# Attention probabilities and merged rows split in SBUF and transposed by DMA, with new planner constants

## Chip, cores and metric

The kernel runs on one core of a Trainium2 chip. The metric is the device time of one execution in microseconds; lower is better. The time of the kernel before is the median of three runs, 1886.96 us (1886.47 to 1887.98).

## The reference

One step of a single-layer encoder over 1024 prompt frames and 32 sample frames of width 1024: a joint input projection, two parallel branches over 8 heads (differential attention and retention), their gated sum, an output projection, a SwiGLU block and a gated per-layer embedding.

```python
qa, ka, va, qr, kr, vr, g_ret, gate_a, gate_r = mix_inputs(x, w_in, ...)   # rmsnorm(x) @ w_in, split
s = jnp.einsum('bqhcd,bkhcd->bhcqk', q_blk, ka) * scale       # two softmax maps per head, c = 0, 1
p = jax.nn.softmax(jnp.where(mask, s, -jnp.inf), axis=-1)
a = p[:, :, 0] - lam * p[:, :, 1]
o = jnp.einsum('bhqk,bkhe->bqhe', a, va)                      # then rmsnorm over the head
...
mix = jax.nn.sigmoid(gate_a) * o_a + jax.nn.sigmoid(gate_r) * o_r
x = x + mix @ w_o
```

## The kernel before

**Arithmetic.** Matmuls keep about float32 accuracy with float16 operands: each operand is a pair, a high part (rounded to float16) and a low part (the rest), and one product takes three matmuls, high by high, high by low and low by high. Splitting a float32 tile into its pair takes two instructions: a scaled copy to float16 on ScalarE or VectorE, and a `scalar_tensor_tensor` on VectorE that multiplies and subtracts.

**Stages.** The first stage, 50 to about 1000 us of the trace, walks 8 heads of 9 units each (8 blocks of 128 prompt frames, and the sample as block 8): 72 units. For each unit `stream` projects two blocks of 512 columns (`project`, lines 748 to 750, 24 matmuls each), one for attention (`unit_a`, then `attend`) and, four units later (`LAG`), one for retention and gates (`unit_b`). The merged rows of a unit go to DRAM (`mix_d`) and come back as `mixs` for the output projection. Later stages (output projection, SwiGLU in 7 products, down projection, embedding gate) aren't touched.

**Attention of one unit** (`attend`). With NK keys (128 for block 0 up to 1024 for block 7; 544 for the sample) and `nb_` = 1 to 8 blocks of values (5 for the sample; 41 in a head): scores on PE into PSUM `sc` (889 to 892), row maximum (899, VectorE), two exponentials into the float32 tiles `pm[0]` and `pm[1]` of the pool `p`, which has 5 buffers (909, ScalarE), the two maps combined into `pm[0]` (923, VectorE). Then TensorE transposes each 128 x 128 block of `pm[0]` into PSUM (938), at most four to a bank; the bank is split into the high and low halves of `aT` (945 on ScalarE or 947 on VectorE, and 949); and the products with the values follow (957, 958, 961), three matmuls per block.

**End of a unit** (`unit_b`). The merged rows `mx` (1240) are transposed by TensorE (1245), split from PSUM into `mixT` (1250, 1252) and stored (1254).

**Transposing DMAs** already turn the queries and keys: the pair is made in SBUF as `qst`, and `nc.sync.dma_start_transpose` on SP's queue writes `q4` (1087, 128 rows x 256 columns, 64 KB) and `kT` (1088, 128 x 512, 128 KB).

**Order.** The instruction order on PE, DVE, ACT and POOL is fixed at build time by a planner, `Flow`: every piece of work is a generator that yields engine and assumed duration (`M` PE, `V` VectorE, `S` ScalarE, `G` GpSimd, `D` the DMA path), takes and returns buffers (`get`, `put`) and waits for events. `Flow` always issues the piece that could start first on its assumed clock. DMAs go to SP's single queue in the order in which the planner reaches them, and SP works through them strictly in order. For a transposing DMA the planner books `xbar(tiles)` on the DMA path and then `landed(tiles)` before the data may be used, a tile being 16 rows of 128 columns.

Of the kernel before, what the change touches and what calls it, by code (L numbers as in the profile page):

```python
# [21 lines left out]
P = 128  # L22
# [48 lines left out]
def M(us):  # L71
    return {"M": us}
# [6 lines left out]
def X(us):  # L79
    return {"D": us}  # L80


def xbar(tiles):

    return 0.5 + 0.027 * tiles


def landed(tiles):

    return ("delay", 2.0 + 0.03 * tiles)  # L90


def either(*ds):
    out = {}
    for d in ds:
        out.update(d)
    return out
# [100 lines left out]
def kernel(  # L198
# [26 lines left out]
    nc = tc.nc  # L225
# [30 lines left out]
    id32 = cst_sb[:, 0, :]  # L256
# [245 lines left out]
    with ExitStack() as pa:  # L502
# [18 lines left out]
        lsc = ca.tile([P, 1], F32, name="lsc")  # L521
# [5 lines left out]
        wk = pa.enter_context(DT(name="wk", bufs=2))  # L527
# [3 lines left out]
        ps_o = pa.enter_context(DT(name="ps_o", bufs=3, space=PSUM))  # L531
# [346 lines left out]
        def attend(key, i, R, q4, sblocks, masked, vblocks, NK, sc_ap, do_ap):  # L878
            pm, Z = [], sm(2, "Z", 6)
            nm = sm(2, "nm", 6)  # L880
            nb = sm(2, "nb", 6)
            for ms in ((0, 1),) if NK <= 512 else ((0,), (1,)):
# [3 lines left out]
                for m in ms:  # L886
                    for b0, n, kts in sblocks:
                        o = ps[0:R, 512 * ms.index(m) + b0:512 * ms.index(m) + b0 + n]
# [32 lines left out]
            p0, p1 = pm[0][0:R, 0:NK], pm[1][0:R, 0:NK]  # L921
            yield V(NK, 1.0, 0.06)
            nc.vector.scalar_tensor_tensor(out=p0, in0=p1, scalar=cz[0:R], in1=p0, op0=ALU.mult, op1=ALU.add)
            yield ("put", "p")
            yield V(1)
            dz = sm(1, "dz", 6)
            nc.vector.tensor_tensor(out=dz[0:R], in0=rz[0:R, 0:1], in1=do_ap[0:R], op=ALU.mult)
            nb_ = len(vblocks)
            yield ("get", "aT")
            aT = wk.tile([P, 2, 8, P], F16, tag="aT", name="aT")  # L930
            for j0 in range(0, nb_, 4):
                js = range(j0, min(j0 + 4, nb_))
                yield ("get", "o")
                yield M(0.107 * len(js))
                pt = ps_o.tile([P, 512], F32, tag="o", name="t").rearrange("p (b c) -> p b c", b=4)
                for j in js:
                    n = vblocks[j][0]
                    nc.tensor.transpose(out=pt[0:n, j - j0, 0:R], in_=pm[0][0:R, j * P:j * P + n], identity=id32[0:R, 0:R])  # L938
                if js[-1] == nb_ - 1:
                    yield ("put", "p")  # L940
                n, nj = vblocks[js[-1]][0], len(js)
                hi = aT[0:n, 0, j0:j0 + nj, 0:R]
                g = yield either(S(nj * R, 0.05), V(nj * R, 1.0, 0.06))
                if g == "S":
                    nc.scalar.activation(hi, pt[0:n, 0:nj, 0:R], AF.Copy, scale=lsc[0:n])
                else:
                    nc.vector.tensor_scalar(out=hi, in0=pt[0:n, 0:nj, 0:R], scalar1=lsc[0:n], scalar2=None, op0=ALU.mult)
                yield V(nj * R, 1.0, 0.06)
                nc.vector.scalar_tensor_tensor(out=aT[0:n, 1, j0:j0 + nj, 0:R], in0=pt[0:n, 0:nj, 0:R], scalar=lsc[0:n], in1=hi,
                                               op0=ALU.mult, op1=ALU.subtract)  # L950
                yield ("put", "o")
            yield ("get", "o")
            yield M(0.165 * nb_)
            po = ps_o.tile([P, 512], F32, tag="o", name="po")[0:R, 0:P]
# [70 lines left out]
        def unit_a(h, i, ps, dA, e):  # L1025
# [57 lines left out]
            yield ("get", "q4")  # L1083
            rows = st[0:R].rearrange("p g a c -> p (g a c)")
            q4 = wk.tile([P, 2, P], F16, tag="q4", name="q4")
            yield X(xbar(6 * RT // 16))
            nc.sync.dma_start_transpose(out=q4[:, :, 0:R], in_=rows[:, 0:256])
            nc.sync.dma_start_transpose(out=kT[:, :, t0:t0 + RT], in_=rows[0:RT, 256:768])
            yield landed(6 * RT // 16)
            yield ("put", "qst")  # L1090
            if i < NT - 1:

# [97 lines left out]
        def unit_b(h, i, ps, dB, e):  # L1190
# [47 lines left out]
            yield ("put", "th")  # L1238
            g = yield either(G(P), V(P))
            ENG[g].tensor_tensor(out=mx[0:R], in0=mx[0:R], in1=of[0:R], op=ALU.add)  # L1240
            yield ("delay", 0.4)
            yield ("get", "o")
            yield M(0.12)
            pt = ps_o.tile([P, 512], F32, tag="o", name="t")
            nc.tensor.transpose(out=pt[:, 0:P], in_=mx, identity=id32)
            pt = pt[:, 0:RT]
            yield ("get", "mix")
            yield S(P, 0.05)
            mt = hp.tile([P, 2, P], F16, tag="mixT", name="mixT", bufs=4)
            nc.scalar.activation(mt[:, 0, 0:RT], pt, AF.Copy, scale=smx)  # L1250
            yield V(P, 1.0, 0.06)
            nc.vector.scalar_tensor_tensor(out=mt[:, 1, 0:RT], in0=pt, scalar=smx, in1=mt[:, 0, 0:RT],
                                           op0=ALU.mult, op1=ALU.subtract)
            nc.sync.dma_start(out=mix_d[h, :, :, t0:t0 + RT], in_=mt[:, :, 0:RT])
            yield ("later", ("mix", 2.2))
            yield ("put", "o")
            yield ("put", "B")
            yield ("set", ("b", h, i))

# [118 lines left out]
        def stream():  # L1378
# [65 lines left out]
            for part in range(4):  # L1444
                flow.add(ple(part), 6)

        flow = Flow(dict(pj=3, sc=1, o=3, p=5, A=5, B=3, w=3, st=2, mix=4, z=3, kv=3, rot=2, sqz=2, qst=2, q4=2, aT=2, of=2,
                         ret=2, th=2, xc=3, su=1))
        flow.buffers["w"].pop()
        with tc.manual_schedule(engines={mybir.EngineType.PE, mybir.EngineType.DVE, mybir.EngineType.Activation,  # L1450
                                         mybir.EngineType.Pool}):
# [645 lines left out]
```

## Time and profile before

| | us |
|---|---|
| median of 3 runs | 1886.96 |
| profiled execution, its own time | 1889.55 |
| its span, first to last instruction | 1887.7 |
| PE busy | 1838.3 |
| DVE busy | 1487.0 |
| ACT busy | 1065.3 |
| POOL busy | 672.5 |

The profile lists for each group of instructions a line, an engine, the tile written and the tiles read, the count, the busy time and the mean length of one, and the idle time of the engine just before them. Consecutive matmuls overlap in their pipeline, so the mean length of one is longer than its share of PE's time; that share is read from the distance of two starts in the timeline. SP's own waits and issues stand in rows of SPq.

### The profile page before, as it was taken

The page shows a single profiled execution, that of the slowest core. Times are in us where ns is not written, and L with a number is a line of the kernel's source. Part 1 is how long each engine was busy: PE and PEld are TensorE (multiplying, and loading weights), DVE is VectorE, ACT ScalarE, POOL GpSimd, SP SyncE. Part 2 cuts the span into 40 slices and gives each one's busy share as a digit, 9 for nine tenths or more (in the row PEclk, how much of TensorE's full clock was granted, in tenths as well). Part 3 has the DMA queues.
Part 4 walks back from the last instruction along what each step waited for, and adds up shares of the span by engine and source line. Part 5 has one row for each costly group of instructions (what it writes and reads, how often), then busy time and mean ns, then how long its engine had stood idle before and what let it go on. Part 6 is the DMA issues. An engine that isn't in the chain of part 4 may idle for free.

```text
span 1887.7 us, 37668 instructions
## 1 busy us (share of the span) xinstructions
PE 1838.3 (97%) x13791; PEld 1196.6 (63%) x13791; DVE 1487.0 (79%) x3874; ACT 1065.3 (56%) x2776; POOL 672.5 (36%) x1137
## 2 busy tenths in 40 slices
PE   6999999999999999999999998999999999999999
PEld 3455555655655556555566686777777776666666
DVE  7888778778887888878887589999999986644364
ACT  7677667676676766767666345656555542201132
POOL 3555445454444454544441266323232300000010
PEclk9999999999999999999999999999999999999999
DMA  5333213123132231322218421222211116212031
GB/s 197 87 92 91 78 40 103 53 72 94 33 90 72 64 100 27 99 74 62 80 44 285 138 66 45 91 92 80 68 46 68 46 63 257 66 59 90 1 135 50
DMA packets 128780, 160.25 MB, mean 85 GB/s; under 512 B 82098, under 2 KB 108978, under 8 KB 120659
## 3 DMA queue, kind: packets, MB, share of 16 engines
q1 hardware_dynamic: 128594, 157.85, 26.6%
q8 instruction: 108, 1.77, 0.4%
q14 instruction: 78, 0.63, 0.1%
HBM read 113.09 MB, written 31.34 MB: 77 GB/s over the span
## 4 chain that ended last, share of the span: by engine, by line
PE 72%; DVE 14%; POOL 6%; ACT 4%; issue 3%; DMA 1%; SPq 0%; POOLq 0%; DVEq 0%; ACTq 0%
PE ps L488 9%; PE ps L489 9%; PE ps L490 9%; PE pj L748 7%; PE pj L750 7%; PE pj L749 7%; PE ps L1486 4%; PE ps L1484 4%; PE ps L1485 4%; PE t L938 1%; PE sc L889 1%; PE sc L892 1%; ACT p L909 1%; PE pj L759 1%; DVE w L1637 1%
## 5 line engine op out<-in xcount | busy, mean ns | idle before, releaser
L748 PE MATMUL pj<-w,xh 128*128 128x512 f16 x1024 | 389.1, 380 | 2.8 <-ACT w L479 2.8
L749 PE MATMUL pj<-w,xh 128*128 128x512 f16 x1024 | 389.0, 380 | 0.6 <-DVE w L481 0.6
L750 PE MATMUL pj<-w,xh 128*128 128x512 f16 x1024 | 388.9, 380 | 0.0
L489 PE MATMUL ps<-mixs,w 128*128 128x352 f16 (+1 forms) x960 | 262.1, 278 | 5.9 <-DVE mixs L1509 5.9
L488 PE MATMUL ps<-mixs,w 128*128 128x352 f16 (+1 forms) x960 | 262.1, 278 | 0.3 <-DVE o1c L244 0.3
L490 PE MATMUL ps<-mixs,w 128*128 128x352 f16 (+1 forms) x960 | 262.1, 278 | 0.0
L490 PEld LDWEIGHTS <-w 128*128 128x128 f16 x1736 | 170.7, 98 | 57.0 <-issue 6.0
L488 PEld LDWEIGHTS <-w 128*128 128x128 f16 x1736 | 171.0, 98 | 55.7 <-issue 4.9
L489 PEld LDWEIGHTS <-w 128*128 128x128 f16 x1736 | 170.7, 98 | 50.2 <-issue 1.2
L750 PEld LDWEIGHTS <-xh 128*128 128x128 f16 x1024 | 100.3, 98 | 122.5 <-issue 2.2
L1642 POOL TENSOR_TENSOR st<-st 128x512 f32<-128x512 f32 x66 | 88.9, 1347 | 244.4 <-DVE w L1637 165.7
L748 PEld LDWEIGHTS <-xh 128*128 128x128 f16 x1024 | 101.5, 99 | 79.2 <-issue 3.0
L749 PEld LDWEIGHTS <-xh 128*128 128x128 f16 x1024 | 100.2, 98 | 76.4 <-issue 3.7
L909 ACT ACTIVATE p<-sc,nb,scs 128x256 f32<-128x256 f32 (+7 forms) x128 | 106.0, 829 | 73.6 <-POOL nb L901 42.7
L488 PE MATMUL ps<-tT,w 128*128 128x352 f16 (+1 forms) x528 | 143.5, 276 | 0.0
L489 PE MATMUL ps<-tT,w 128*128 128x352 f16 (+1 forms) x528 | 143.4, 276 | 0.0
L490 PE MATMUL ps<-tT,w 128*128 128x352 f16 (+1 forms) x528 | 143.4, 276 | 0.0
L1637 DVE SCALAR_TENSOR_TENSOR w<-st,gus,w 128x512 f16<-128x512 f32 x132 | 138.2, 1047 | 0.1
L899 DVE TENSOR_REDUCE nm<-sc 128x1 f32<-128x640 f32 (+6 forms) x112 | 102.8, 918 | 15.5 <-PE sc L892 14.4
L1486 PE MATMUL ps<-a,w 128*128 128x352 f16 x312 | 97.5, 313 | 0.5 <-DVE w L1728 0.5
L1484 PE MATMUL ps<-a,w 128*128 128x352 f16 x312 | 97.5, 313 | 0.0
L1485 PE MATMUL ps<-a,w 128*128 128x352 f16 x312 | 97.5, 313 | 0.0
(427 smaller groups left out, 4741.7 us busy)
## 6 DMA issues: line engine op xcount, KB each, us to landing
st<-in_win_dram SPq DMA_DIRECT2D x30, 1024.0 KB, 5.0
st<-in_wgu_dram SPq DMA_DIRECT2D x22, 1024.0 KB, 4.9
st<-in_wdn_dram SPq DMA_DIRECT2D x16, 704.0 KB, 4.9
out_dram<-kv SPq DMA_DIRECT2D x64, 128.0 KB, 1.7
a_d<-a SPq DMA_DIRECT2D x9, 528.0 KB, 2.6
b<-a_d SPq DMA_DIRECT2D x9, 528.0 KB, 7.7
mixs<-mix_d SPq DMA_DIRECT2D x8, 528.0 KB, 7.1
pw_d<-pws SPq DMA_DIRECT2D x12, 352.0 KB, 5.1
```

The costliest lines, as they stand in the source:

```text
L488: nc.tensor.matmul(out=ps, lhsT=wh, rhs=ah, start=first, stop=False)
L489: nc.tensor.matmul(out=ps, lhsT=wh, rhs=al, start=False, stop=False)
L490: nc.tensor.matmul(out=ps, lhsT=wl, rhs=ah, start=False, stop=last)
L748: nc.tensor.matmul(out=ps, lhsT=xhi, rhs=w[:, k, 0], start=(k == 0), stop=False)
L749: nc.tensor.matmul(out=ps, lhsT=xhi, rhs=w[:, k, 1], start=False, stop=False)
L750: nc.tensor.matmul(out=ps, lhsT=xh[:, k, 1, t0:t0 + P], rhs=w[:, k, 0], start=False, stop=(k == KD - 1))
L899: nc.vector.tensor_reduce(out=nm[0:R, mc], in_=pv, axis=AX.X, op=ALU.max, negate=True)
L909: nc.scalar.activation(pt[0:R, 0:NK], ps[0:R, p0:p0 + NK], AF.Exp, bias=nb[0:R, m:m + 1], scale=sc_ap[0:R], accum_out=Z[0:R, m:m + 1])
L1484: nc.tensor.matmul(out=ps, lhsT=wt[:, 0, j], rhs=a[:, 0, cs], start=(first and j == js[0]), stop=False)
L1485: nc.tensor.matmul(out=ps, lhsT=wt[:, 1, j], rhs=a[:, 0, cs], start=False, stop=False)
L1486: nc.tensor.matmul(out=ps, lhsT=wt[:, 2, j], rhs=a[:, 1, cs], start=False, stop=(last and j == js[-1]))
L1637: nc.vector.scalar_tensor_tensor(out=w[:, i, 1], in0=src, scalar=s, in1=w[:, i, 0], op0=ALU.mult, op1=ALU.subtract)
```

## The change

In `attend`, the combined map in `pm[0]` is split in SBUF: the float16 halves go side by side into the memory of `pm[1]`, which is free once the maps are combined, and one transposing DMA turns all blocks, high and low, into `aT`. The 328 PE transposes of a run (41 for each of 8 heads) go, and 72 DMAs of 2 x `nb_` blocks come. `pm[1]` now returns to the pool only when the DMA has landed, `pm[0]` when the low half is written. In `unit_b` the merged rows are split into a new tile `ms` (2 buffers) and turned by a DMA of 64 KB; the 72 PE transposes go, and the store to `mix_d` waits for that DMA. The fixed delay of 0.4 ahead of the old transpose goes. The planner's `xbar` and `landed` get other numbers, for the query and key DMAs too, which are now booked as two pieces.

```diff
 def xbar(tiles):
-    return 0.5 + 0.027 * tiles
+    return 1.15 + 0.006 * tiles
 def landed(tiles):
-    return ("delay", 2.0 + 0.03 * tiles)
+    return ("delay", 1.3 + 0.02 * tiles)
@@ attend
+            NB = nb_ * P
+            pf = pm[1].bitcast(F16)
+            hi, lo, src = pf[0:R, 0:NB], pf[0:R, NB:2 * NB], pm[0][0:R, 0:NB]
+            g = yield either(S(NB, 0.05), V(NB, 1.0, 0.06))
+            if g == "S":
+                nc.scalar.activation(hi, src, AF.Copy, scale=lsc[0:R])
+            else:
+                nc.vector.tensor_scalar(out=hi, in0=src, scalar1=lsc[0:R], scalar2=None, op0=ALU.mult)
+            yield V(NB, 1.0, 0.06)
+            nc.vector.scalar_tensor_tensor(out=lo, in0=src, scalar=lsc[0:R], in1=hi, op0=ALU.mult, op1=ALU.subtract)
+            yield ("put", "p")
             yield ("get", "aT")
-            for j0 in range(0, nb_, 4):
-                yield M(0.107 * len(js))
-                for j in js:
-                    nc.tensor.transpose(out=pt[0:n, j - j0, 0:R], in_=pm[0][0:R, j * P:j * P + n], identity=id32[0:R, 0:R])
...
-                nc.vector.scalar_tensor_tensor(out=aT[0:n, 1, j0:j0 + nj, 0:R], in0=pt[0:n, 0:nj, 0:R], scalar=lsc[0:n], in1=hi,
+            yield X(xbar(2 * nb_ * R // 16))
+            nc.sync.dma_start_transpose(out=aT.rearrange("p a j c -> p (a j) c")[:, :, 0:R], in_=pf[0:R, 0:2 * NB])
+            yield landed(2 * nb_ * R // 16)
+            yield ("put", "p")
@@ unit_a
-            yield X(xbar(6 * RT // 16))
+            yield X(xbar(2 * R // 16))
             nc.sync.dma_start_transpose(out=q4[:, :, 0:R], in_=rows[:, 0:256])
+            yield X(xbar(4 * RT // 16))
             nc.sync.dma_start_transpose(out=kT[:, :, t0:t0 + RT], in_=rows[0:RT, 256:768])
-            yield landed(6 * RT // 16)
+            yield landed(4 * RT // 16)
@@ unit_b
-            yield ("delay", 0.4)
-            yield M(0.12)
-            nc.tensor.transpose(out=pt[:, 0:P], in_=mx, identity=id32)
+            nc.scalar.activation(ms[:, 0], mx, AF.Copy, scale=smx)
+            nc.vector.scalar_tensor_tensor(out=ms[:, 1], in0=mx, scalar=smx, in1=ms[:, 0], op0=ALU.mult, op1=ALU.subtract)
+            yield X(xbar(2 * RT // 16))
+            nc.sync.dma_start_transpose(out=mt[:, :, 0:RT], in_=ms[0:RT].rearrange("p a c -> p (a c)"))
+            yield landed(2 * RT // 16)
+            yield X(0.05)
             nc.sync.dma_start(out=mix_d[h, :, :, t0:t0 + RT], in_=mt[:, :, 0:RT])
```

Since the planner sets the order anew, rows move on every engine. Three places show it. First SP's queue in the third head, where blocks 5 and 6 are under way; of before (weight load, store of keys and values, the two DMAs of queries and keys, two stores of merged rows):

```order
L421 DMA st<-in_win_dram 128x2048
L1063 DMA out_dram<-kv 128x256
L1087 DMA_TRANSPOSE q_5354<-qst 128x2x128
L1088 DMA_TRANSPOSE kT<-qst 128x4x128
L1254 DMA mix_d<-mixT 256x1x128 x2
```

And of the changed kernel at that place (L942 turns the probabilities, with 2 x `nb_` as the middle size, L1244 the merged rows, L1248 stores them, L1056 stores keys and values):

```order
L942 DMA_TRANSPOSE aT<-p 128x10x128
L942 DMA_TRANSPOSE aT<-p 128x12x128
L1056 DMA out_dram<-kv 128x256
L1244 DMA_TRANSPOSE mixT<-ms 128x2x128
L1080 DMA_TRANSPOSE q_5464<-qst 128x2x128
L1082 DMA_TRANSPOSE kT<-qst 128x4x128
L1248 DMA mix_d<-mixT 256x1x128
L942 DMA_TRANSPOSE aT<-p 128x14x128
```

The queue holds two DMAs more for each unit, and the probabilities of one unit now stand behind stores and turns of other units. Over the whole program the store of merged rows stands directly behind its own transposing DMA in 28 of 72 units.

Second PE in the sixth head, around the products of block 0; of before:

```order
L750 MATMUL pj<-w,xh 128x512
L314 LDWEIGHTS cst_sb
L314 MATMUL mt<-wamh,cst_sb 128x1
L957 LDWEIGHTS aT
L957 MATMUL po<-vh,aT 128x128
L958 LDWEIGHTS aT
L958 MATMUL po<-vh,aT 128x128
L961 LDWEIGHTS aT
L961 MATMUL po<-vh,aT 128x128
L1245 MATMUL t<-cst_sb,mx 128x128
```

And of the changed kernel there (L950, L951 and L954 are the products):

```order
L750 MATMUL pj<-w,xh 128x512
L950 LDWEIGHTS aT
L950 MATMUL po<-vh,aT 128x128
L951 LDWEIGHTS aT
L951 MATMUL po<-vh,aT 128x128
L954 LDWEIGHTS aT
L954 MATMUL po<-vh,aT 128x128
L759 LDWEIGHTS w
```

The products are the same; no transpose stands among them any more, neither of merged rows (L1245) nor of probabilities.

Third DVE in the fifth head, block 2, from the combination of the maps to the low half; of before:

```order
L923 SCALAR_TENSOR_TENSOR p<-p,cz 128x384
L1169 TENSOR_TENSOR inn<-pr,cst_sb 128x128
L927 TENSOR_TENSOR dz<-rz,dop 128x1
L947 TENSOR_SCALAR aT<-t,lsc 128x384
L1181 TENSOR_TENSOR S_134<-s_136,pr 64x128
L949 SCALAR_TENSOR_TENSOR aT<-t,lsc,aT 128x384
```

And of the changed kernel:

```order
L923 SCALAR_TENSOR_TENSOR p<-p,cz 128x384
L1177 TENSOR_SCALAR S_134<-S_134 64x128
L926 TENSOR_TENSOR dz<-rz,dop 128x1
L1046 TENSOR_REDUCE qss<-sqz 128x4
L935 TENSOR_SCALAR p<-p,lsc 128x384
L1009 SCALAR_TENSOR_TENSOR vh<-pj,vh 128x128
L937 SCALAR_TENSOR_TENSOR p<-p,lsc 128x384
```

The split now reads and writes SBUF (`p`) where it read PSUM (`t`), and it comes in one piece of all columns: 72 low halves (L937) in place of 112, and 30 of the high halves on DVE (L935) with 42 on ACT.

More of the change, by code (lines that the diff above doesn't have):

```diff
@@ L923, in attend @@
             nc.vector.scalar_tensor_tensor(out=p0, in0=p1, scalar=cz[0:R], in1=p0, op0=ALU.mult, op1=ALU.add)
-            yield ("put", "p")
             yield V(1)
@@ L928, in attend @@
             nb_ = len(vblocks)
-            yield ("get", "aT")
-            aT = wk.tile([P, 2, 8, P], F16, tag="aT", name="aT")
-            for j0 in range(0, nb_, 4):
-                js = range(j0, min(j0 + 4, nb_))
-                yield ("get", "o")
-                yield M(0.107 * len(js))
-                pt = ps_o.tile([P, 512], F32, tag="o", name="t").rearrange("p (b c) -> p b c", b=4)
-                for j in js:
[L937 to L951, printed above, removed]
@@ L952, in attend @@
+            yield ("put", "p")
+            yield ("get", "aT")
+            aT = wk.tile([P, 2 * 8 * P], F16, tag="aT", name="aT")[:, 0:2 * NB].rearrange("p (a j c) -> p a j c", a=2, c=P)
+            yield X(xbar(2 * nb_ * R // 16))
+            nc.sync.dma_start_transpose(out=aT.rearrange("p a j c -> p (a j) c")[:, :, 0:R], in_=pf[0:R, 0:2 * NB])
+            yield landed(2 * nb_ * R // 16)
+            yield ("put", "p")
             yield ("get", "o")
@@ L1240, in unit_b @@
             ENG[g].tensor_tensor(out=mx[0:R], in0=mx[0:R], in1=of[0:R], op=ALU.add)
-            yield ("delay", 0.4)
-            yield ("get", "o")
-            yield M(0.12)
-            pt = ps_o.tile([P, 512], F32, tag="o", name="t")
-            nc.tensor.transpose(out=pt[:, 0:P], in_=mx, identity=id32)
-            pt = pt[:, 0:RT]
+            yield ("get", "ms")
+            yield S(P, 0.05)
+            ms = wk.tile([P, 2, P], F16, tag="ms", name="ms")
+            nc.scalar.activation(ms[:, 0], mx, AF.Copy, scale=smx)
+            yield V(P, 1.0, 0.06)
+            nc.vector.scalar_tensor_tensor(out=ms[:, 1], in0=mx, scalar=smx, in1=ms[:, 0], op0=ALU.mult, op1=ALU.subtract)
             yield ("get", "mix")
-            yield S(P, 0.05)
             mt = hp.tile([P, 2, P], F16, tag="mixT", name="mixT", bufs=4)
[L1250 to L1253, printed above, removed]
+            yield X(xbar(2 * RT // 16))
+            nc.sync.dma_start_transpose(out=mt[:, :, 0:RT], in_=ms[0:RT].rearrange("p a c -> p (a c)"))
+            yield landed(2 * RT // 16)
+            yield ("put", "ms")
+            yield X(0.05)
             nc.sync.dma_start(out=mix_d[h, :, :, t0:t0 + RT], in_=mt[:, :, 0:RT])
             yield ("later", ("mix", 2.2))
-            yield ("put", "o")
             yield ("put", "B")
@@ L1447 @@
         flow = Flow(dict(pj=3, sc=1, o=3, p=5, A=5, B=3, w=3, st=2, mix=4, z=3, kv=3, rot=2, sqz=2, qst=2, q4=2, aT=2, of=2,
-                         ret=2, th=2, xc=3, su=1))
+                         ret=2, th=2, xc=3, su=1, ms=2))
         flow.buffers["w"].pop()
```

## Prediction

> **What bounds the kernel now.** I read the page's busy shares and its 40 slices first, then a table by stretches of the first stage, then the groups of instructions.
>
> ```profile
> PE 1838.3 (97%) x13791; PEld 1196.6 (63%) x13791; DVE 1487.0 (79%) x3874; ACT 1065.3 (56%) x2776; POOL 672.5 (36%) x1137
> PE   6999999999999999999999998999999999999999
> 770.00:890.00 120.00, 118.62 (x850) 69.93 (x849) 98.76 (x300) 82.76 (x247) 55.68 (x117) 1.00 0.26 72
> 50.00:998.00 948.00, 932.73 (x6626) 547.51 (x6625) 778.97 (x2351) 655.76 (x1947) 454.05 (x927) 1.00 0.26 72
> ```
>
> The columns of the last two rows are the stretch, then PE, PEld, DVE, ACT and POOL busy, granted clock, DMA share and GB/s. In the stage that the change touches PE is busy 118.62 of 120 us at full clock, DVE 98.76, ACT 82.76, and the DMA engines a quarter. PE's order is fixed, so an instruction that goes from PE gives back its share of PE's time, as long as nothing else arrives later than PE then comes to it.
>
> **What goes from PE.** Start-to-start distances, since matmuls overlap:
>
> ```profile
> L938 PE MATMUL t<-cst_sb,p 128*128 128x128 f32 x328 | 54.4, 274 | 1.4 <-DVE p L923 1.1 <-DVE aT L949 0.2
> L1245 PE MATMUL t<-cst_sb,mx 128*128 128x128 f32 x72 | 20.5, 284 | 4.8 <-POOL mx L1240 2.7 <-DVE mx L1240 1.8
> 985.06 0.60 PE L938 MATMUL t<-cst_sb,p 128*128 128x128 f32 x4
> 985.49 0.38 PE L889 MATMUL sc<-kcs,q 128*128 128x512 f16 x1
> 644.71 0.28 PE L1245 MATMUL t<-cst_sb,mx 128*128 128x128 f32 x1
> 644.83 0.38 PE L748 MATMUL pj<-w,xh 128*128 128x512 f16 x1
> ```
>
> Four transposes take 985.49 - 985.06 = 0.43 us, 0.108 each; one of merged rows takes 0.12. So 328 x 0.108 + 72 x 0.12 = 35.4 + 8.6 = **44.0 us** of PE time go, and with them the listed idle time ahead of them, 1.4 + 4.8 = 6.2 us, which may come back at the next waiting instruction.
>
> **What DVE and ACT get.** The low half of the probabilities stays one DVE instruction per element, from SBUF in place of PSUM:
>
> ```profile
> L949 DVE SCALAR_TENSOR_TENSOR aT<-t,lsc,aT 128x512 f16<-128x512 f32 x54 | 40.0, 743 | 2.5 <-ACT aT L945 2.3
> L923 DVE SCALAR_TENSOR_TENSOR p<-p,cz 128x512 f32<-128x512 f32 x8 | 6.0, 750 | 0.2
> L923 DVE SCALAR_TENSOR_TENSOR p<-p,cz 128x1024 f32<-128x1024 f32 x8 | 10.3, 1284 | 0.2
> L909 ACT ACTIVATE p<-sc,nb,scs 128x1024 f32<-128x1024 f32 x16 | 19.2, 1201 | 4.4 <-POOL nb L901 4.4
> ```
>
> The form from SBUF costs the same at 512 columns (750 against 743 ns), and one of 1024 (1284) replaces two of 512 (1486), so DVE loses a little work, and with 30 instead of 54 high halves on it a little more. At 98.76 of 120 it has room for a head that is 5.5 us shorter (44.0 / 8). The merged rows keep their two instructions. I book nothing for DVE and ACT; PE hides both, and if it did not, DVE at 98.76 would only bind a stretch cut from 120 us to under 99.
>
> **What SP and the DMA engines get.** The kernel already has two transposing DMAs per unit, which give issue and landing:
>
> ```profile
> L1087 SPq DMA_TRANSPOSE q<-qst x72: 1167/1195/2177, 43.1 to 978.0; - x72
> L1088 SPq DMA_TRANSPOSE kT<-qst x72: 1170/1216/2066, 44.5 to 979.3; - x72
> q<-qst SPq DMA_TRANSPOSE x72, 2.3
> kT<-qst SPq DMA_TRANSPOSE x72, 2.4
> 645.95 1.21 SPq L1088 DMA_TRANSPOSE kT<-qst  x1
> 647.00:647.50 0.50, 0.50 (x4) 0.28 (x2) 0.48 (x2) 0.50 (x2) 0.00 (x0) 1.00 0.61 127
> 647.50:648.00 0.50, 0.50 (x6) 0.47 (x6) 0.35 (x1) 0.50 (x2) 0.00 (x0) 1.00 1.58 125
> ```
>
> SP is held 1.2 us by either, 64 or 128 KB, and they land 2.3 and 2.4 us after the issue began. A merged-row DMA is the size of `q`: 1.2 held, 2.3 to land. One of the probabilities has 64 KB per block of values, so 64 to 512 KB. No row shows 512 KB, so its landing is bounded: by the step from `q` to `kT` (0.1 us for 64 KB) it is 2.3 + 7 x 0.1 = 3.0 us; by the two stretches, in which the 128 KB of `kT` took about 1.0 us from about 1.05 us after its issue, it is 1.05 + 4 x 1.0 + 0.3 = 5.4 us. I take 3.9, nearer the landings measured whole. Load on the DMA engines: (0.61 + 1.58) x 0.5 = 1.1 us of all 16 for 128 KB; 41 x 64 KB + 9 x 64 KB = 3.2 MB per head make 27 us, some 24% of a head, on top of 0.26. Not a bound.
>
> The Trainium skill, "Advanced Engine Details and Errata", section X-Bar Transpose (TRN2), expects 350-400 GB/s; an estimate from it is 1.4 us of transfer for 512 KB, which would put the landing near the lower bound, where the stretches above show 127 GB/s over half a microsecond; the lower landing would raise the forecast's chance and leave its sum.
>
> **Does PE reach the products before the data?** The new chain from the last score to the products of block 7 (1024 keys), out of the rows above and these:
>
> ```profile
> L899 DVE TENSOR_REDUCE nm<-sc 128x1 f32<-128x1024 f32 x16 | 19.5, 1219 | 1.6 <-PE sc L892 1.5
> L909 ACT ACTIVATION_READ_ACCUMULATOR p<-sc,nb,scs 128x1 f32 x128 | 25.0, 195 | 0.0
> L919 DVE SCALAR_TENSOR_TENSOR cz<-rz,nlam,Z 128x1 f32<-128x1 f32 x71 | 18.6, 261 | 1.2
> L916 DVE RECIPROCAL rz<-Z 128x2 f32<-128x2 f32 x71 | 11.5, 162 | 29.1 <-ACT p L909 28.3
> L901 DVE TENSOR_SCALAR nb<-nm,scs 128x1 f32<-128x1 f32 x20 | 4.1, 206 | 0.2
> L899 DVE TENSOR_REDUCE nm<-sc 128x2 f32<-128x256 f32 x8 | 3.4, 422 | 1.9 <-PE sc L892 1.2 <-PE mt L314 0.6
> L909 ACT ACTIVATE p<-sc,nb,scs 128x128 f32<-128x128 f32 x16 | 7.3, 456 | 11.9 <-DVE nb L901 8.8 <-POOL nb L901 2.3 <-DVE B1p L248 0.8
> L923 DVE SCALAR_TENSOR_TENSOR p<-p,cz 128x128 f32<-128x128 f32 x8 | 2.9, 361 | 0.2
> 645.48 0.38 PE L748 MATMUL pj<-w,xh 128*128 128x512 f16 x1
> ```
>
> Maximum 1.22, bias 0.21, exponential 1.20 + 0.20, reciprocal and factor 0.42, combination 1.28, high half 1.20 (as an exponential of that width), low half 1.28, landing 3.9: 10.9 us, 10.0 to 12.4 by the bounds. Counting PE's rows between that unit's last score and first product in the new order, each at its start-to-start distance (0.217 for a projection, (645.48 - 644.83) / 3, and 0.108 for a float32 transpose), PE has 15.0 us of work there (median of heads 2 to 8, the least 11.2), against 12.0 before. For block 0 (64 KB) the same chain with the short forms (0.42 maximum, exponentials of 0.46 + 0.20 twice, 0.36 for each later step) makes about 6 us, and PE has 9.0 (8.0 at least) against 5.5 before. So the order leaves 3 to 4 us for queueing, where block 0 of before, with a chain of 3.7, had 1.8. And these were PE's waits in the stage at products and scores with that:
>
> ```profile
> PE sc L889 <- ACT p L909: 1.9, 2, 1.5
> PE po L957 <- DVE aT L947: 0.9, 1, 0.9
> PE po L957 <- DVE aT L949: 0.4, 1, 0.4
> ```
>
> In all 72 units the scores never waited on a landing. What the new wait at the products costs in all isn't shown: it is nothing if SP keeps the planner's order, and 72 times the mean overshoot if not. I take 0.1 us a unit, **7 us**, since the few waits above total 3.2 us and SP is now in the path. What stands behind a waiting product in PE's queue is the next projection, so an overshoot is lost in full.
>
> **The end of the stage.** The last merged rows now go through a DMA of 2.3 us in place of a transpose of 0.3 before the store and the reload. Before, the output projection began behind a weight load, not behind them:
>
> ```profile
> 1021.54 0.32 SPq L1376 DMA_DIRECT2D mixs<-mix_d x1
> 1025.96 0.69 DVE L440 TENSOR_REDUCE wam<-st 128x2 f32<-128x512 f32 x1 [3.49 <-DMA st<-in_wo_dram]
> 1030.89 0.47 PE L488 MATMUL ps<-mixs,w 128*128 128x352 f16 x1 [0.26 <-DVE o1c L244]
> ```
>
> I book 2 us; if all is hidden, 0. The table of issue and landing times for `q` and `kT` is part of the same order and costs nothing by itself.
>
> **Sum.** The profiled execution took 1889.55 us (span 1887.7), 2.6 above the median 1886.96. -44.0 - 6.2 + 7 + 2 = -41 us: 1848 beside the profile's time, **1846** beside the median.
>
> **Rivals.**
> 1. *Large turns are dear.* If SP's hold grows with size as bytes do, 512 KB hold SP 4 x 1.2 = 4.8 us and land no sooner than 6; the chain of block 7 becomes 7.0 + 6 = 13 of PE's 15.0, the queue has 2 us a unit more, and a mean overshoot that I put at 0.4 us in 72 units takes 29 us in place of the 7: 1846 + 22 = 1868. For it: no row shows a turn over 128 KB. Against: doubling the size cost 21 ns.
> 2. *SP's order turns on the change.* SP works in order, and behind a late item everything is late:
>
> ```profile
> SPq L1063 <- POOL kv L1062: 282.0, 59, 8.5
> SPq L1087 <- DVE qst L1077: 51.0, 39, 3.5
> ```
>
> The store of keys and values held SP 59 times, 282.0 / 59 = 4.8 us each; before, only work that came later anyway stood behind it. Now turned probabilities do, and a store of merged rows that waits 2.3 - 1.2 = 1.1 us for its own turn. A product caught behind both is 5.9 us late, less the 3 to 4 us of room: 2.4 us. If two units in three are caught, 48 x 2.4 = 115 us of stall stand against 48 us: 1886.96 - 50 + 2 + 115, about 1954; if half of that, 1896. It decides from a mean overshoot of 0.67 us a unit (48 / 72). For it: the numbers of the row. Against: in 39 units SP stood waiting for the queries themselves, so it kept up with the planner's order.
>
> The Trainium skill, "VectorE: DVE Perf Modes", Rules for kernel authors, speaks against the change: for a 128 x 128 transpose it names TensorE if PSUM will do, the crossbar otherwise. By that rule the longer path would show as waits, and the time would be rival 2's; the trace has 0.108 us of a busy PE against 2.3 us of a queue that scores have never waited for.
> 3. *The change doesn't do what it says*, because PE isn't the bound: then the stage stays 948 us long and the time within 0.2%. 118.62 of 120 us speaks against it.
>
> **How the numbers follow.** Forecast 1846 (1836 to 1857): 0.58; rival 1 (1857 to 1883): 0.20; rival 3 (same): 0.05; rival 2 (slower): 0.17. The low end is -50 with no new wait at all. With the high end at 1884, 0.22 lies above and some 0.01 below, so I reach a little into rival 3 and the mild half of rival 2: 1834 to 1892. Faster by over 0.2% (about what a measurement of this kernel can tell from no change) 0.78, within 0.05, slower 0.17.
>
> **What would show it.** Right: PE busy in the first stage again at 98 to 99% of a stage near 905 us; no transposes of probabilities in the list; waits of PE at the products (L950) under 10 us in all; probabilities landing 2.3 to 4 us after issue, SP held about 1.2 to 1.4 by each. Rival 1: SP held several microseconds by the large ones. Rival 2: waits at L950 of 50 us or more, and SP rows in which L942 stands behind L1056 or L1248. The forecast is wrong if PE's idle time in the stage exceeds some 20 us.

## The result, and the profile after

| | median, us | runs | ratio to before, 95% interval |
|---|---|---|---|
| before | 1886.47 | 1883.87 to 1887.98 (5) | |
| changed | 1896.78 | 1893.62 to 1899.95 (5) | 1.0058 (1.0042 to 1.0074) |

The changed kernel is 0.6% slower; the forecast was 2.2% faster. Its profiled execution took 1898.33 us with a span of 1896.5. First the busy time of each engine, its share of the span and its instructions, of the changed kernel:

```profile
PE 1808.5 (95%) x13391; PEld 1152.9 (61%) x13391; DVE 1474.4 (78%) x3784; ACT 1063.3 (56%) x2762; POOL 715.1 (38%) x1161
```

PE is 29.8 us less busy than in before (1838.3), and yet the span is 8.8 us longer: PE has got idle time. Where, the table by stretches tells. Its columns are the stretch, PE, PEld, DVE, ACT and POOL busy, granted clock, DMA share, GB/s. Before:

```profile
50.00:950.00 900.00, 884.77 (x6252) 517.11 (x6251) 739.09 (x2241) 625.30 (x1859) 436.25 (x886) 1.00 0.26 73
950.00:1050.00 100.00, 97.08 (x743) 63.33 (x742) 72.54 (x210) 58.41 (x159) 23.05 (x54) 0.97 0.55 185
```

Changed:

```profile
50.00:950.00 900.00, 851.73 (x5862) 474.58 (x5860) 722.70 (x2141) 621.80 (x1842) 473.79 (x906) 0.99 0.42 99
950.00:1050.00 100.00, 90.63 (x676) 55.73 (x674) 72.89 (x214) 58.56 (x161) 29.18 (x58) 0.95 0.63 185
```

Up to 950 us PE stands idle 900 - 851.73 = 48.3 us against 15.2, and at the end of the stage 9.4 against 2.9: 39.5 us of new idle time against 44.0 us of work removed. The clock is lower too. The prediction's own sign of being wrong, more than some 20 us of idle time in the stage, is there. The output projection, whose first matmul started at 1030.89 in before, starts here:

```profile
1038.95 0.47 PE L488 MATMUL ps<-mixs,w 128*128 128x352 f16 x1 [0.25 <-DVE o1c L244]
```

8.1 us later; what follows takes as long as before within 1 us, so the loss lies ahead of that row. Of PE's waits in the changed kernel (time in all, times, longest) the first row is the largest, and the second is the one that matters later:

```profile
PE po L950 <- DMA aT<-p: 23.9, 16, 4.5
...
PE sc L889 <- DMA kT<-qst: 3.1, 3, 1.3
```

How the DMAs of the probabilities issued (SP's hold in ns: least, median, most) and landed, from the view of that line:

```profile
L942 SPq DMA_TRANSPOSE aT<-p x72: 1175/1350/2691, 63.3 to 997.1; - x72
DMA to landing us min/median/max: 2.3/3.7/7.7
```

Sixteen products waited, 23.9 us in all. The longest of these waits, from the timeline of the changed kernel:

```profile
661.03 1.21 SPq L1080 DMA_TRANSPOSE q<-qst  x1
661.59 0.48 DVE L937 SCALAR_TENSOR_TENSOR p<-p,lsc 128x256 f16<-128x256 f32 x1
662.34 2.02 SPq L1082 DMA_TRANSPOSE kT<-qst  x1
664.45 0.54 SPq L421 DMA_DIRECT2D st<-in_win_dram  x1
665.08 1.20 SPq L942 DMA_TRANSPOSE aT<-p  x1
670.41 0.29 PE L950 MATMUL po<-vh,aT 128*128 128x128 f16 x1 [4.52 <-DMA aT<-p]
```

The low half was ready at 661.59 + 0.48 = 662.07. SP first turned keys (2.02 us) and issued a weight load of 1 MB, came to the probabilities 3.0 us late, and these took 5.3 us to land behind the load. Two causes offer themselves at once, a landing that is late behind a load and SP's order. They work together: of the sixteen turns that were waited for, SP came to thirteen more than 1 us after the low half was ready, and seven, with 14.9 of the 23.9 us, had a weight load issued less than 4 us ahead of them. The experiments try them one by one.

### The profile page after: what moved, and what is told of

It reads as the page before. It is cut to its first block, busy times and chain, and to the rows that moved or that the text cites. A ratio compares the mean times of both kernels' runs of the same rounds, so it can differ in the third digit from the quotient of the medians.

```text
span 1896.5 us, 37208 instructions
## 1 busy us (share of the span) xinstructions
PE 1808.5 (95%) x13391; PEld 1152.9 (61%) x13391; DVE 1474.4 (78%) x3784; ACT 1063.3 (56%) x2762; POOL 715.1 (38%) x1161
## 4 chain that ended last, share of the span: by engine, by line
PE 58%; DVE 17%; POOL 8%; ACT 7%; DMA 5%; issue 4%; SPq 0%; POOLq 0%; DVEq 0%; ACTq 0%
PE ps L488 9%; PE ps L490 9%; PE ps L489 9%; PE ps L1479 4%; PE pj L748 4%; PE pj L749 4%; PE ps L1478 4%; PE pj L750 4%; PE ps L1477 4%; DMA aT<-p 3%; ACT p L909 2%; DVE nm L899 2%; POOL qkr L784 2%; DVE w L481 1%; DVE w L1630 1%
## 5 line engine op out<-in xcount | busy, mean ns | idle before, releaser
L750 PE MATMUL pj<-w,xh 128*128 128x512 f16 x1024 | 390.4, 381 | 0.0
L750 PEld LDWEIGHTS <-xh 128*128 128x128 f16 x1024 | 100.5, 98 | 123.5 <-issue 3.8
L909 ACT ACTIVATE p<-sc,nb,scs 128x896 f32<-128x896 f32 (+7 forms) x128 | 106.3, 831 | 87.6 <-POOL nb L901 52.5
```

Of the source, the lines that this page charges most:

```text
L750: nc.tensor.matmul(out=ps, lhsT=xh[:, k, 1, t0:t0 + P], rhs=w[:, k, 0], start=False, stop=(k == KD - 1))
L909: nc.scalar.activation(pt[0:R, 0:NK], ps[0:R, p0:p0 + NK], AF.Exp, bias=nb[0:R, m:m + 1], scale=sc_ap[0:R], accum_out=Z[0:R, m:m + 1])
```

## The experiments

All ratios are to before, run on the same chip beside each. Kernels that ran at different times compare best by these ratios, since before itself had medians from 1886.47 to 1889.26 us.

**Parts and table.** First the two halves of the change alone, and its planner's numbers alone. The theories that the expectations name: A, probabilities land late behind 1 MB loads; B, SP's own queue holds up what stands behind a waiting store; C, the new numbers make a worse order.

```diff
# e1: merged rows back on PE; e2: probabilities back on PE; e3: both
-            nc.sync.dma_start_transpose(out=mt[:, :, 0:RT], in_=ms[0:RT].rearrange("p a c -> p (a c)"))
+            nc.tensor.transpose(out=pt[:, 0:P], in_=mx, identity=id32)
...
-            nc.sync.dma_start_transpose(out=aT.rearrange("p a j c -> p (a j) c")[:, :, 0:R], in_=pf[0:R, 0:2 * NB])
+                    nc.tensor.transpose(out=pt[0:n, j - j0, 0:R], in_=pm[0][0:R, j * P:j * P + n], identity=id32[0:R, 0:R])
```

> The probabilities by DMA as in the change, the merged rows back on PE, the new table of issue and landing times kept. PE slots removed against before: 328 x 0.108 = 35.4 us. Theory A (turns of probabilities that stand behind a 1 MB load land late, and PE stalls there and loses its clock): the loss stays, 1888 to 1900 us. Theory B (SP's own order: the merged rows' turn and the store that waits 60 us for it hold up everything behind them on SP): without them the gain of 35 us comes back in large part, 1855 to 1870. Theory C (the new table alone makes a worse order): as A here, so E3 has to tell.

> The merged rows by DMA as in the change, the probabilities back on PE, the new table kept. PE slots removed against before: 72 x 0.12 = 8.6 us. Theory A: the rows' turns are waited for by no engine but SP, so about -8 us, 1876 to 1882. Theory B: SP waits about 60 us for the rows' own landing and holds up q and k turns behind it, 1888 to 1900. Theory C: above 1890.

> Both transposes back on PE; only the table of issue and landing times and the split booking of q's and k's turns are new. No work differs from before, only the order. Theories A and B: within 0.3% of before, 1882 to 1892. Theory C (the new numbers make a worse order): slower, 1895 to 1905.

Measured: probabilities alone 1881.34 us, 0.9970 (0.9958 to 0.9981); merged rows alone 1900.72, 1.0072 (1.0059 to 1.0085); table alone 1888.81, 1.0005 (0.9996 to 1.0015). C falls. The small part, 8.6 us of PE's slots, is the one that loses: slower by 13.9 us (1900.72 against 1886.84 beside it). In its trace PE waits for keys, which the change hardly touches; of its waits:

```profile
PE sc L889 <- DMA kT<-qst: 12.9, 6, 3.7
```

And its timeline at one of the six (lines 1087 and 1089 turn queries and keys, 1255 stores merged rows in this kernel):

```profile
175.87 0.28 DVE L1077 TENSOR_TENSOR qst<-z,qst 128x128 f16<-128x128 f32 x1
176.94 0.52 SPq L421 DMA_DIRECT2D st<-in_win_dram  x1
179.56 0.57 SPq L1255 DMA_DIRECT2D mix_d<-mixT  x1
180.24 1.22 SPq L1087 DMA_TRANSPOSE q<-qst  x1
182.18 1.22 SPq L1089 DMA_TRANSPOSE kT<-qst  x1
185.28 0.32 PE L889 MATMUL sc<-kT,q 128*128 128x384 f16 x1 [3.66 <-DMA kT<-qst]
```

Queries and keys were ready at 176.15. SP had issued the load by 177.46 and then stood at the store of merged rows, which waited for its own turn, until 179.56; the queries went out 4.1 us late and PE stood 3.66 us. SP's waits at this store are 62.4 us in 51 places. That is theory B.

The probabilities alone gained, but 5.5 of the 35.4 us. At 950 us this kernel is ahead: of the projections (L750) the groups of PE's rows between 950 and 1040 us show 46 left in before, 31 here. First before, then probabilities alone:

```profile
L750 PE MATMUL pj<-w,xh 128*128 128x512 f16 x46 | 17.4, 379 | 0.0
```

```profile
L750 PE MATMUL pj<-w,xh 128*128 128x512 f16 x31 | 11.7, 379 | 0.0
```

Counting those that started between 50 and 950 us gives the same, 962 against 947. Fifteen projections at 900 / 947 = 0.95 us are 14 us. Much of the lead is lost at the end of the stage, in the timeline of probabilities alone:

```profile
1007.39 0.46 SPq L421 DMA_DIRECT2D st<-in_wo_dram  x1
1016.78 0.69 DVE L440 TENSOR_REDUCE wam<-st 128x2 f32<-128x512 f32 x1 [7.08 <-DMA st<-in_wo_dram]
```

and in its table by stretches (the clock is the last column but two):

```profile
1010.00:1020.00 10.00, 2.53 (x13) 1.13 (x10) 3.12 (x9) 1.03 (x2) 0.00 (x0) 0.71 0.92 324
1020.00:1030.00 10.00, 8.98 (x39) 5.11 (x38) 7.41 (x27) 6.09 (x15) 0.00 (x0) 0.60 0.60 196
```

PE waited 7.5 us for the last 1 MB of weights, which landed 9.4 us after their issue, with the DMA engines 0.92 busy, and worked at a lower clock after it. This is theory E below: the end of the stage is a chain of its own.

**The loads on another queue.**

```diff
             yield DM(1.0)
-            nc.sync.dma_start(out=st, in_=src)
+            nc.scalar.dma_start(out=st, in_=src)
             yield ("delay", 3.0)
```

> The changed kernel with one edit: the 1 MB loads of the weights are issued on ACT's queue in place of SP's, so that a turn does not stand behind a load in one queue. [...] Theory A, if the lateness comes of standing in one queue: the landing of the probabilities' turns stays under 5 us, the waits at the products fall from 24 to under 12 us and the clock stays at 1.0, 1870 to 1885. Theory A, if the DMA engines themselves are shared without regard to the queue: landing up to 7 us as before, 1892 to 1900. Theory B: SP is freed of 2 us in some places only, 1890 to 1900.

Measured: 1924.82 us, 1.0201 (1.0187 to 1.0215), 28 us worse than the change. From its trace, the landing of the probabilities:

```profile
DMA to landing us min/median/max: 2.3/3.9/9.8
```

Another queue doesn't bring the turns ahead of a load: they land later still, and PE's waits for them rise from 23.9 to 29.9 us. The turn that took 9.8 us was issued at 639.60 us and the load only after it, at 640.14, on the other queue. The four loads of the last weights, in ScalarE's order now, were issued between 985.9 and 1049.5 us, after 932.3 to 1026.4 in the change; how the 28 us divide between the two was not tried. The Trainium skill, "Trainium Kernel Development and Optimization", section Key Constraints, says that the DMAs of the SP, ACT and POOL queues run on the same 16 engines and interleave, and that several queues save only issue time; a longest landing of 9.8 against 7.7 us agrees.

**The store later, and what the order is.** Theory B was tried by placing the store of merged rows 4 us later in the planner, in the change and in rows alone (D in the expectations: the rows cost by their share of the DMA engines).

```diff
             yield ("put", "ms")
+            yield ("put", "B")
+            yield ("delay", 4.0)
             yield X(0.05)
             nc.sync.dma_start(out=mix_d[h, :, :, t0:t0 + RT], in_=mt[:, :, 0:RT])
             yield ("later", ("mix", 2.2))
-            yield ("put", "B")
```

> The changed kernel with the store of each unit's merged rows put 4 us later in the planner's order (the buffer of the unit is given back ahead of it), so that SP no longer stands at it while its own turn lands. Theory B (SP's order: those waits of 60 us in 44 places hold up the turns of q, k and the probabilities behind them): the waits of SP there fall under 15 us and the time goes by 10 to 20 us under the changed kernel's 1897, to 1877 to 1887. Theory A (turns late behind 1 MB loads): little moves, 1892 to 1898. Theory D (the rows' turns cost by their share of the 16 DMA engines, not by SP's order): 1892 to 1898 too, with the waits of SP gone.

> The kernel with only the merged rows by DMA, with the same later store. Theory B: the 13 us of PE's waits for k's turn and the clock lost behind them go, from 1900.7 to 1878 to 1886 (8.6 us of PE's slots are gone against before). Theory D: stays at 1895 to 1902.

Measured: 1898.60 us, 1.0056 (1.0043 to 1.0068), and 1901.37, 1.0070 (1.0056 to 1.0084): nothing. But the edit had not done what it says; SP's waits at the store (line 1250 here) are as before, in the first of the two:

```profile
SPq L1250 <- DMA mixT<-ms: 66.5, 46, 5.1
```

SP's queue in the program shows why: between a turn of merged rows and its store stand 1.07 other DMAs on the mean in the change, and 1.13 here. The planner does not set SP's order. The code fixes the order of four engines, and SP isn't among them, in before and in the change:

```
with tc.manual_schedule(engines={mybir.EngineType.PE, mybir.EngineType.DVE, mybir.EngineType.Activation,
                                 mybir.EngineType.Pool}):
    flow.add(stream(), 3)
    flow.run()
```

So the sentence on SP in the part on the kernel, that DMAs go to its queue in the order in which the planner reaches them, is wrong, and the prediction rested on it. The two runs tell nothing on B.

**More room in the plan, and the last weights first**, both with the probabilities alone:

```diff
# e7
-                        flow.add(load_wo_0(), 1)
+                        flow.add(load_wo_0(), -3)
                         for j in range(2):
-                            flow.add(load_wo_1(j), 0)
+                            flow.add(load_wo_1(j), -3)
# e8
             yield landed(2 * nb_ * R // 16)
+            yield ("delay", 3.0)
```

> The kernel with only the probabilities by DMA, with the four loads and splits of the last weights put ahead of all other work in the planner (priority -3 in place of 1 and 0). In the run without this edit PE waited 7.5 us at the end of the first stage for the last 1 MB of these weights, 12 us at a lower clock with it, while it had been some 24 us ahead of before by projections at 850 us. Theory E (the end of the first stage is a chain of its own, which takes back what PE has gained): 1868 to 1876. If the gain is lost earlier, 1879 to 1884.

> The kernel with only the probabilities by DMA, with the planner told that such a turn lands 3 us later than in the change's table, so that other matmuls are ordered between. Theory A (the table is short of what turns take behind loads, and PE stalls): waits at the products fall from 5.8 us to under 2, 1874 to 1880. If those waits are not where the time is: 1880 to 1886, or above it, since the chain of each unit gets longer and the buffers of scores and probabilities are held longer.

Measured: 1878.92 us, 0.9954 (0.9941 to 0.9966), against 0.9970 without the edit: a gain of 2 us that the intervals don't separate. More room: 1888.13, 0.9999 (0.9990 to 1.0007), 7 us worse, though the waits at the products fell from 5.8 to 2.6 us. Those waits aren't where this kernel's time is, and a longer chain costs more than they did.

**SP in the planner's order.** Theory F, that the turns are late by SP's order, was tried with this edit alone on four kernels (the change, with the later store, probabilities alone, before):

```diff
         with tc.manual_schedule(engines={mybir.EngineType.PE, mybir.EngineType.DVE, mybir.EngineType.Activation,
-                                         mybir.EngineType.Pool}):
+                                         mybir.EngineType.Pool, mybir.EngineType.SP}):
```

> The changed kernel with SP added to the engines whose order the planner fixes; the orders on PE, VectorE, ScalarE and GpSimd stay the same to the row, only that of SP differs. In the change and in before SP is not on that list, and its order of DMAs is not the planner's. Theory F (the turns' lateness is one of SP's order, which the planner believes it sets and doesn't): the waits at the products fall from 24 to under 12 us, 1875 to 1888. Theory B (stores ahead of turns cost, whoever sets the order): the stores stand as close as before, 1890 to 1900. Theory A (DMA engines full behind 1 MB loads): 1890 to 1900 too.

> As the run before, and the store of merged rows 4 us later in the planner's order, which now binds SP. Theory B: SP's waits for the rows' own landing fall from 60 us to under 15, and the time to 1865 to 1880. Theory A or D: within 5 us of the run with SP planned alone.

> Only the probabilities by DMA, SP's order by the planner. Theory F: 1868 to 1877 against 1881 without; if SP's order matters to the rows' part alone: 1878 to 1884.

> Before, with SP's order by the planner and nothing else: the control. Every theory: within 0.3% of before, 1881 to 1893, since PE waits for almost no DMA in it.

| | SP's order as it was | by the planner |
|---|---|---|
| before | 1 | 1.0046 (1.0034 to 1.0058) |
| probabilities alone | 0.9970 (0.9958 to 0.9981) | 1.0007 (0.9998 to 1.0016) |
| the change | 1.0058 (1.0042 to 1.0074) | 1.0013 (1.0005 to 1.0022) |
| the change, store 4 us later | 1.0056 (1.0043 to 1.0068) | 0.9983 (0.9975 to 0.9992) |

In the changed kernel nothing differs but SP's order, row for row (466 of its 700 places hold another DMA), and it gets 4 us faster by the medians (1892.79) and some 8 by the ratios. That is less than theory F expected (1875 to 1888). At the place of the 4.52 us wait its timeline reads:

```profile
655.01 2.22 SPq L942 DMA_TRANSPOSE aT<-p  x1
657.32 0.54 SPq L1182 DMA_DIRECT2D out_dram<-S  x1
657.92 1.27 SPq L1082 DMA_TRANSPOSE kT<-qst  x1
659.24 0.57 SPq L421 DMA_DIRECT2D st<-in_win_dram  x1
```

and PE's waits for landings:

```profile
PE sc L889 <- DMA kT<-qst: 14.1, 14, 3.0
...
PE po L950 <- DMA aT<-p: 3.9, 4, 1.8
```

The probabilities go ahead of the keys and the load, and the waits at the products fall from 23.9 to 3.9 us, as theory F says. Theory A isn't refuted by it. The longest wait that is left follows a turn that SP issued 0.08 us after its low half, right behind a load, and that landed 6.8 us later:

```profile
624.48 0.60 SPq L421 DMA_DIRECT2D st<-in_win_dram  x1
625.24 1.26 SPq L942 DMA_TRANSPOSE aT<-p  x1
632.05 0.23 PE L950 MATMUL po<-vcs,aT 128*128 128x128 f16 x1 [1.80 <-DMA aT<-p]
```

A load delays the turn behind it in either order; SP's order decides how many turns stand behind one, and how late SP comes to them. The waits for keys, however, rise from 3.1 to 14.1 us. With the store later as well, now that the planner binds SP, its waits there fall to 10.5 us, those of PE for keys to 7.9 and for probabilities to 1.6:

```profile
SPq L1250 <- DMA mixT<-ms: 10.5, 7, 4.7
```

The time is 1886.48 us, 10 us under the change (14 by the ratios), which speaks for theory B, though it expected 1865 to 1880. The control went against every theory: before gets 0.5% slower. Its trace shows PE waiting 7.6 us for the last weights (1.8 in before). Probabilities alone get slower too, against theory F. There the wait for the last weights is no longer than without the edit (6.4 against 7.5 us), but PE's waits for keys rise from 1.2 to 7.4 us. So the planner's order isn't better for SP as such: it serves the probabilities, and it delays keys and, in before, the last weights.

**What is left.** Both turns by DMA, SP by the planner, the store later, and the last weights ahead as in e7 (e13); then the store of keys and values later, with e14 on e13 and e15 on probabilities alone; then the third load of the last weights earlier, on e14 (e16) and on before (e17).

```diff
# e14, e15
-            nc.sync.dma_start(out=kvo[h, t0:t0 + RT], in_=kv[0:RT])
-            yield ("later", ("kv", 3.0))
+            def store_kv():
+                yield ("delay", 3.0)
+                yield X(0.05)
+                nc.sync.dma_start(out=kvo[h, t0:t0 + RT], in_=kv[0:RT])
+                yield ("later", ("kv", 3.0))
+            flow.add(store_kv(), 0)
# e16, e17
                 yield from load_block_steps(wo[j], w, j, None, "o", mixun, d)
-            yield ("set", "wo0")
+                yield ("set", "wo0" if j else "wo0a")
...
-            yield ("wait", "wo0")
+            yield ("wait", "wo0" if j else "wo0a")
```

> Both turns by DMA, SP by the planner, the rows' store 4 us later, and the last weights' loads and splits ahead of other work. Theory E (the stage's end takes back some 10 us): PE's wait of 6.5 us for the last weights goes and the clock stays up there, 1873 to 1880 against 1886.5. If the end of the stage is bound by the last units' own chains: 1883 to 1888.

> As the run before, and the store of each unit's keys and values 3 us later in the planner's order. Theory B for this store (SP stands 111 us in 41 places at it, with k's turn behind it): SP's waits there fall under 30 us, PE's waits for k's turns from 8 to under 2 us, and the time goes 4 to 10 us under the run before. If SP's waits there only fill time in which nothing else is ready: within 3 us of it.

> Only the probabilities by DMA, SP by the planner, the last weights ahead, the store of keys and values 3 us later. Without the last two edits 1890.7. Theories B and E together: 1868 to 1877. If the merged rows on PE cost no more than their 8.6 us of slots, this is slower than the run before by 3 to 9 us; if their chain by DMA costs more than it frees, faster.

> As the run with both stores later, and the third of the four loads of the last weights may be issued when the first is split, not the second, so that only one load is left at the end of the stage. Theory E (the gain up to 950 us is lost at the stage's end, where PE waits for these weights): PE's wait of 6.2 us goes, 1869 to 1876 against 1878.9. If another chain ends the stage there: 1877 to 1882.

> Before with the same edit and the same priority of the last weights. Before has 1.8 us of PE's waits at that place, so every theory: within 4 us of before. If it is faster by more, the gain of the run above is not one of the change.

| | median, us | ratio to before, 95% interval |
|---|---|---|
| e13, last weights ahead | 1885.79 | 0.9991 (0.9982 to 1.0001) |
| e14, store of keys and values later | 1878.88 | 0.9952 (0.9939 to 0.9964) |
| e15, the same, probabilities alone | 1887.23 | 0.9997 (0.9988 to 1.0006) |
| e16, e14 and third load earlier | 1877.27 | 0.9932 (0.9918 to 0.9946) |
| e17, before and third load earlier | 1887.28 | 0.9990 (0.9981 to 0.9999) |

Priority alone did nothing (e13, PE still waits 6.2 us at the end). The second store is worth 7 us between e13 and e14: SP's waits there (120.5 us in 42 places in e13) go, and SP waits for what it should, the queries (lines 1085 and 1087 turn queries and keys here). Waits of SP and of PE in e14:

```profile
SPq L1085 <- DVE qst L1075: 90.8, 38, 8.0
...
PE sc L889 <- ACT p L909: 7.7, 10, 1.8
PE pr L1162 <- DVE qT L402: 7.0, 8, 1.5
PE por L1170 <- DVE inn L1168: 6.5, 9, 1.8
...
PE sc L889 <- DMA kT<-qst: 4.4, 3, 3.0
...
PE po L950 <- DMA aT<-p: 0.9, 3, 0.5
```

and its two stretches:

```profile
50.00:950.00 900.00, 865.09 (x6030) 484.31 (x6029) 734.58 (x2200) 632.90 (x1869) 479.04 (x911) 1.00 0.43 100
950.00:1050.00 100.00, 90.00 (x643) 57.17 (x642) 64.16 (x186) 49.20 (x132) 19.03 (x39) 0.97 0.73 229
```

PE's longest waits are now for other engines' results and no longer for landings.

With SP's order put right the merged rows by DMA gain 8.4 us between e15 and e14, about what their slots are worth (8.6 removed). That the two agree so well is partly luck: the profiled executions differ by 11.7 us, and 5.6 of these are clock. The probabilities alone gain nothing over before in this order (e15, 0.9997, where theories B and E expected 1868 to 1877 us). In e16 the wait for the last weights is gone, and the run is the fastest of all, 0.68% under before and 0.58% under before with the same edit (0.9932 / 0.9990). Yet it is only 1.6 us under e14, the intervals overlap, and its expectation had put that down to "another chain": the stretch from 950 to 1050 us has 8.7 us of PE idle in place of 10.0, now spread over waits for the results of ScalarE and VectorE. So E holds as far as the place of the loss goes; one late load was not its whole cause.

One control is missing. Before was run with SP by the planner alone (0.5% slower) and with the early weights alone (0.1% faster), but not with these and the later store of keys and values together. So it stays open how much of the gain of e14 and e16 over before the transposes bring by themselves.

## Why the prediction was wrong

By its steps:

1. *PE bounds the stage, and 44.0 us of its slots go.* Right, and the size too: taken from start to start over all rows, the transposes held PE for 36.9 + 8.7 = 45.6 us in before. Where less clock is lost (e14), PE is busy 1798.8 us, 39.5 less than in before.
2. *Nothing for DVE and ACT, since PE hides both.* Their busy times are right: 1474.4 and 1063.3 us, both a little less. The hiding isn't complete: up to 950 us PE's waits for results of DVE, ACT and POOL rose from 14.4 us to 20.8 in the change, and to 28.8 in e14. POOL's busy time rose from 672.5 to 715.1, which wasn't foreseen and which no run isolates.
3. *SP held 1.2 us, landing 3.9 for the largest.* The middle is right: 1.35 held, 3.7 landed. The tail isn't: 2.7 held and 7.7 landed at most. The load on the DMA engines was booked as a mean, and the mean stayed low (0.42); it hides that a turn behind a load lands late. Rival 1 (large turns dear) falls.
4. *The wait at the products, 0.1 us a unit, 7 us.* **This is the step that failed.** It was 23.9 us, and its reason failed with it: "it is nothing if SP keeps the planner's order", and SP "kept up" with that order. SP has an order of its own. In the planner's, the waits at the products are 3.9 us, under the 7 booked. But the time is then 1892.79 us and not 1846: this step is 17 of the 50 us by which the forecast missed, and steps 2, 5, 6 and 8 hold much of the rest.
5. *The merged rows as a gain of 8.6 us without a wait.* Failed by the same premise: alone they cost 13.9 us, with 12.9 us of PE's waits for keys, because the store that waits for their landing holds the keys of the next unit. The prediction had that wait in rival 2, but only with probabilities behind it. With both stores out of the way they gain 8.4.
6. *2 us at the end of the stage.* Too small: PE's idle time there rose by 6.5 us in the change, by 8.7 with the probabilities alone (88.39 busy of 100). More than half of the lead of 14 us that these had went there, where PE waited for the last loads.
7. *The table costs nothing.* Right: 1.0005.
8. *The clock* stood in no term. By the stretches at half clock PE lost 16.0 us in the change and 8.4 in before, so 7.6 more; 7.3 and 1.7 of it lie up to 950 us.

Put together for the profiled executions: the prediction's terms for PE's idle time come to 7 + 2 - 6.2 = +2.8 us, and it rose by 38.6 (33.0 up to 950 us, 6.5 at the end of the stage, -0.9 elsewhere). So the change is -44.0 of slots + 38.6 + 7.6 of clock = +2.2, and measured is +8.8. Most of the other 6.6 us stands in PE's rows right ahead of its idle times: a projection that the next one follows takes 0.217 us of PE from start to start, and one ahead of an idle time is counted with its whole length of 0.38. By rows this makes 5.2 us more than in before, with 88 idle times in place of 56 (the ends of matmuls are modelled in the profile, so this is an estimate), and 1.4 us stay unexplained. For e14 the same sum is -44.0 + 28.1 of idle time - 0.6 of clock + 3.3 ahead of idle times = -13.2, measured -11.4.

Rival 2 has the right time in its milder half (1896) and the right engine, but at a wrong price, so the time is luck. It decided at 0.67 us a unit of lateness at the products and measured 23.9 / 72 = 0.33, and its sign of 50 us of waits there didn't come; the rest came through keys, the end of the stage and the clock. Its other sign did come: 31 of the 72 turns of probabilities stand directly behind a store of merged rows or of keys and values. Rival 3 is half true after the fact: in e14 only 5.1 us of PE's waits for landings are left up to 950 us, and yet PE has 20 us more idle time there than in before, 14.4 of them in short waits for other engines, mostly for exponentials, `qT` and `inn`. I read this as other engines' chains taking up what PE has given up; no run isolates it, and how much of it a better order could win back was not tried. The Trainium skill's rule on 128 x 128 transposes ("VectorE: DVE Perf Modes", Rules for kernel authors: TensorE if PSUM will do) came out right for the change as written, 1.0058. The 0.9952 of e14 goes against it, as far as that can be compared with a before whose stores stand otherwise.

## What to carry to other kernels

Before moving work to a queue, find out who orders that queue: a planner that fixes four engines doesn't order the fifth, and an edit of its numbers that leaves a queue's rows where they were is no test. A store that waits for the landing of a DMA ahead of it in the same in-order queue charges its wait to everything behind it, so place it where its data have landed. Work taken off the bounding engine is worth its slots only until the next chain; look for the stage's end, where a lead has nothing to be spent on.

## What the runs showed of the hardware

**Short idle times cost clock, but their length alone doesn't decide.** At each of the changed kernel's three longest waits at the products (2.33, 4.09 and 4.52 us) the granted clock fell to a half; at that of 2.20 us it did not. Two of them in the timeline of PE:

```profile
302.07 0.29 PE L950 MATMUL po<-vh,aT 128*128 128x128 f16 x1 [2.33 <-DMA aT<-p]
...
599.09 0.23 PE L950 MATMUL po<-vh,aT 128*128 128x128 f16 x1 [2.20 <-DMA aT<-p]
```

and the stretches behind the three long ones (which ended at 302.07, 670.41 and 111.82) and behind the one of 2.20:

```profile
304.00:306.00 2.00, 2.00 (x39) 1.94 (x38) 0.77 (x2) 1.77 (x8) 0.71 (x3) 0.50 0.75 295
...
674.00:676.00 2.00, 2.00 (x6) 0.66 (x5) 1.69 (x4) 1.04 (x3) 0.46 (x1) 0.50 0.00 0
...
114.00:116.00 2.00, 2.00 (x8) 0.81 (x8) 1.37 (x5) 0.37 (x2) 1.64 (x4) 0.50 0.14 33
...
600.00:602.00 2.00, 2.00 (x15) 0.99 (x13) 0.35 (x1) 1.35 (x6) 0.58 (x2) 1.00 0.32 98
```

The half clock lasted from 300.7 to 307.6, from 669.4 to 676.2 and from 113.0 to 116.4. In it PE worked 5.5, 5.8 and 3.4 us, of which half is lost, 7.3 us. Other traces set no length of wait above which the clock falls. In e14 it stayed up after 2.99 us and fell after 1.75:

```profile
749.96 0.22 PE L889 MATMUL sc<-kT,q 128*128 128x128 f16 x1 [2.99 <-DMA kT<-qst]
750.00:752.00 2.00, 2.00 (x17) 1.37 (x17) 1.35 (x3) 0.79 (x3) 0.74 (x1) 1.00 0.35 103
...
768.78 0.49 PE L1170 MATMUL por<-vr,inn 128*128 128x128 f32 x2 [1.75 <-DVE inn L1168]
770.00:772.00 2.00, 2.00 (x18) 0.90 (x16) 1.15 (x5) 0.53 (x3) 1.50 (x3) 0.50 0.50 128
```

With the loads on ScalarE's queue it stayed at 1.00 even after waits of 3.54 and 3.76 us, and in before it fell behind two waits of 0.95 and 0.89 us that lie 1.9 us apart. The Trainium skill, "TensorE: Matmul & The Clock Gate", section Why this matters for your kernels, warns of idle gaps above some 3 us. The waits of 4.09 and 4.52 us agree; the drops at 2.33 (with another wait of 0.87 us some 3 us ahead of it) and 1.75 us came earlier than that, and at 3.54 and 3.76 us none came.

**A turn by DMA shares its landing with loads, whatever the queue**: 2.3 us at the least, 7.7 at the most with the loads ahead on SP's queue, 9.8 with them on ScalarE's. In the changed kernel a turn with a load of 1 MB close ahead of it landed after 5.4 us in the median of 8, the others after 3.6.
